# Beta's logarithm in the exponent of the decays, one tile of three decay matrices per head, and two 256-column products per chunk in place of four

## The chip, the cores and the metric

The kernel runs on one core of one Trainium2 chip. The core has a tensor engine (PE, with its weight loads PEld), a vector engine (DVE), a scalar engine (ACT), GpSimd (POOL) and a sync engine whose queue issues the DMAs (SP). They share SBUF, and PE writes to PSUM. Each engine runs its own instructions in order. The metric is the device time of one execution in microseconds; lower is better. All data is float32.

## The reference

Two layers of a diffusion backbone over 512 latent and 256 context tokens of width 1024. A layer norms and modulates the tokens, projects them, runs three mixers side by side (windowed attention, a gated DeltaNet in both directions, a Fourier mixing), merges them by gates, and ends with a squared-ReLU MLP. The change is in the DeltaNet, which has 4 heads of 128 channels. Cut to what it touches:

```python
g = jnp.cumsum(g, axis=-1)                       # log-decay within a chunk
decay = where(lower, exp(g[..., :, None] - g[..., None, :]), 0)
kb = k * beta[..., None]
a_mat = where(strict, einsum('cd,sd->cs', kb, k) * decay, 0) + eye
u, w = solve(a_mat, [v * beta, kb * exp(g)])     # unit lower triangular
qk = einsum('cd,sd->cs', qs, k) * decay          # qs = q / sqrt(128)
# scan over chunks, S the state:
v_new = u - w @ S
o = (qs * exp(g)) @ S + qk @ v_new
S = S * exp(g_last) + (k * exp(g_last - g)).T @ v_new
```

beta is a sigmoid. The backward direction is the same on flipped tokens. The kernel works with chunks of 128 tokens: 4 latent and 2 context chunks, so 6 per head.

## The kernel before, in words

A layer has three stages: a first one with the decay gates, the Fourier mixing and the first head's inputs; the mixing stage; and a main stage with gates, output projection and MLP. The mixing stage is where the changed code runs. Four Python generators are interleaved there by a nominal clock (`by_clock`): `stream_dn` runs the scan steps of a head, `stream_prep` the preparation of one head after another (`dn_prep`), `stream_na` the attention, and `stream_in` the input projections of later heads, of the attention and of 16 gate tiles. What they issue is then ordered by a planner that knows dependences, priorities and its own estimates of durations; the order on each engine, SP's queue included, is fixed before the run. Every instruction waits there for what it needs and holds what stands behind it on its engine.

Projections (`proj`, line 255) split their weights in two parts: ACT casts a weight tile to `whi` (line 243), and in the mixing stage POOL makes the remainder `wlo` (line 246), both after SP has loaded `wr` (line 240).

`gates` (from line 415) computes per token and direction the log-decay, its cumulative sum `gc` and its negative `ngc`, `beta` and products of them, as small tiles of 128 x 6 x 8; `gc` goes to DRAM (`gdr`) so that a head's row can be broadcast to all partitions.

`dn_prep` for one head, in order:
1. It takes three tiles `Df`, `Db`, `Dl` (128 x 768) from a pool `pr` with three slots, and SP loads `Df` and `Db` from `gdr` (lines 542 and 543).
2. POOL adds or subtracts the masks: `Dl` from `Df`, then `Db`, then `Df` in place (lines 549 to 551).
3. ACT takes 18 exponentials of 128x128, three per chunk, with `gc` or `ngc` as bias (lines 556 to 558).
4. For each chunk PE computes k k^T and, where there are queries, k q^T into one PSUM tile (lines 564 and 566; this PSUM tag has one buffer, shared with the later steps), and DVE multiplies them by the decays and by beta into `N` and `PT` (lines 567 to 573). In layer 1 the two context chunks have no query.
5. The diagonal 32x32 blocks of `N` go through DRAM to `Nb`, an identity is loaded to `Wb` (both in slots of `pr` again), and 31 pairs of DVE instructions invert them (lines 591 and 593). The result goes back through DRAM into `N` and `Tst`.
6. PE and ACT merge the inverses from 32 to 64 and from 64 to 128 (lines 612 to 649) with a work tile `R`, the sixth tile from `pr`; lines 643 and 645 read `R` last. ACT and DVE then copy the result to `L` (lines 652 and 653), from which the scan steps work. `N` and `L` have one buffer.

A slot of `pr` is taken again as soon as the tile in it has no reader left: the next head's `Df` comes to the slot of `Nb`, its `Db` to that of `Wb`, its `Dl` to that of `R`.

The queries `qT` and keys `kT` of a head come from `dn_in` and `l2_rope`, where POOL multiplies a rotated copy (line 505) and DVE adds (line 507). `dn_step` (from line 657) uses `PT[:, d, j]` at line 704.

Of the kernel before, what the change touches and what calls it, by code (L numbers as in the profile page):

```python
# [11 lines left out]
AF = mybir.ActivationFunctionType  # L12
# [5 lines left out]
P = 128  # L18
# [7 lines left out]
NU = 12  # L26
# [20 lines left out]
def kernel(ctx: ExitStack, tc: tile.TileContext, A: dict, out: bass.AP):  # L47
# [18 lines left out]
    def U(name, dt=F32, tag="u", w=TT):  # L66
        b, n = cur[tag]
        return b.tile([P, w], dt, tag=tag, bufs=n, name=name)
# [4 lines left out]
    @contextmanager  # L73
    def scope(name, **bufs):
        with tc.tile_pool(name=name, bufs=1, reuse_waits="tile") as b:
            for t, n in bufs.items():
                cur[t] = (b, n)
            yield b
# [42 lines left out]
    pool.memset(Tst, 0.0)  # L121
    def sigmoid_into(dst, src):

        act.activation(out=dst, in_=src, func=AF.Abs)
        act.activation(out=dst, in_=dst, func=AF.Exp, scale=-1.0)
        act.activation(out=dst, in_=dst, func=AF.Ln, bias=1.0)
        dve.scalar_tensor_tensor(dst, in0=src, scalar=0.0, in1=dst, op0=ALU.min, op1=ALU.subtract)
        act.activation(out=dst, in_=dst, func=AF.Exp)

# [245 lines left out]
    def layer(l):  # L375
# [39 lines left out]
        def gates():  # L415
# [8 lines left out]
            abv = pab[:, 0:96].rearrange("p (j c) -> p j c", c=16)  # L424
            for nm in ("z", "g", "beta", "gc", "tot", "egc", "tail", "etot", "t0", "nbe", "btail", "ngc"):
                G[nm] = sm.tile([P, 6, 8], F32, tag="g_" + nm, name="g_" + nm)
# [11 lines left out]
                                     op0=ALU.mult, op1=ALU.mult)  # L438
            sigmoid_into(G["beta"], abv[:, :, 8:16])
            pg = ps_aux("ps_g")  # L440
# [6 lines left out]
            act.copy(G["tot"], pgv[:, 2])  # L447
            dve.tensor_scalar(G["ngc"], G["gc"], -1.0, None, op0=ALU.mult)
            act.activation(out=G["egc"], in_=G["gc"], func=AF.Exp)
            act.activation(out=G["etot"], in_=G["tot"], func=AF.Exp)  # L450
# [84 lines left out]
        def dn_prep(h, st):  # L535
            kT, qT = st["kT"], st["qT"]
            v3 = lambda t: t.rearrange("p (j c) -> p j c", c=P)
            src = gdr.rearrange("(j d h) c -> h d j c", d=2, h=4)[h]
            Df = v3(U("Df", tag="pr", w=768))
            Db = v3(U("Db", tag="pr", w=768))  # L540
            Dl = v3(U("Dl", tag="pr", w=768))
            sp.dma_start(out=Df, in_=src[0].unsqueeze(0).to_broadcast([P, 6, P]))
# [9 lines left out]
            for j in range(6):  # L552
                gf = G["gc"][:, j, h:h + 1]
                ngf = G["ngc"][:, j, h:h + 1]
                ngb = G["ngc"][:, j, 4 + h:5 + h]
                act.activation(out=Dl[:, j], in_=Dl[:, j], func=AF.Exp, bias=gf, scale=-1.0)
                act.activation(out=Df[:, j], in_=Df[:, j], func=AF.Exp, bias=ngf)
                act.activation(out=Db[:, j], in_=Db[:, j], func=AF.Exp, bias=ngb)
            yield 6
            for j in range(6):  # L560
                q = full or j < 4
                tk = kT[:, j * P:(j + 1) * P]
                ps = ps_aux("ps_kk", "pp")
                pe.matmul(ps[:, 0:P], lhsT=tk, rhs=tk, start=True, stop=True)
                if q:
                    pe.matmul(ps[:, P:2 * P], lhsT=tk, rhs=qT[:, j * P:(j + 1) * P], start=True, stop=True)
                dve.scalar_tensor_tensor(N[:, 0, j], in0=ps[:, 0:P], scalar=G["beta"][:, j, h:h + 1], in1=Dl[:, j],
                                         op0=ALU.mult, op1=ALU.mult)
                dve.scalar_tensor_tensor(N[:, 1, j], in0=ps[:, 0:P], scalar=G["beta"][:, j, 4 + h:5 + h], in1=Db[:, j],
                                         op0=ALU.mult, op1=ALU.mult)  # L570
                if q:
                    dve.tensor_tensor(PT[:, 0, j], ps[:, P:2 * P], Df[:, j], op=ALU.mult)
                    dve.scalar_tensor_tensor(PT[:, 1, j], in0=ps[:, P:2 * P], scalar=G["beta"][:, j, 4 + h:5 + h],
                                             in1=Db[:, j], op0=ALU.mult, op1=ALU.mult)
                yield 1.2
# [3 lines left out]
            for b in range(4):  # L579
                s = slice(32 * b, 32 * b + 32)  # L580
                sp.dma_start(out=nd[b].rearrange("u i j -> i u j"), in_=Nu[s, :, s])
            Nb = U("Nb", tag="pr", w=1024)[0:48].rearrange("p (i j) -> p i j", j=32)
            sp.dma_start(out=Nb, in_=nd.rearrange("b u i j -> (b u) i j"))
            Wb = U("Wb", tag="pr", w=1024)[0:48].rearrange("p (i j) -> p i j", j=32)
            sp.dma_start(out=Wb, in_=A["eye32"])
# [19 lines left out]

            R = U("R", tag="pr", w=NU * 64).rearrange("p (u c) -> p u c", c=64)

# [49 lines left out]
        def dn_step(h, st, d, step):  # L657
# [36 lines left out]
            if has_q:  # L694
# [3 lines left out]
                if S is not None:  # L698
# [4 lines left out]
                    first = False  # L703
                pe.matmul(ps[:, 0:P], lhsT=st["PT"][:, d, j], rhs=Uc, start=True, stop=True)  # L704
                if first:
# [348 lines left out]
        cur["dve_lo"] = 0  # L1054
        mix_b = scope("mixb", n=8, N=1, PT=2, L=1, pr=3, sp=7, S=3, s6=6, vb=1, Pm=2, bias=2, stmp=1)
        mix_b.__enter__()
# [310 lines left out]
```

## Time and profile before

| | us |
|---|---|
| median of 3 runs | 2640.64 (2636.08 to 2641.43) |
| profiled execution | 2641.14, of which the span in the trace is 2639.4 |
| busy: PE, DVE, ACT, POOL | 2460.9, 1516.9, 1194.3, 652.1 |
| mean granted clock of PE | 0.974 |

The span runs from the first to the last instruction. The mixing stage of layer 0 lies between about 140 and 740 us, that of layer 1 between about 1600 and 2110 us. Durations of one instruction are in ns in the groups by line and in us elsewhere. A bracket behind an instruction is the idle time of its engine just before it, and what ended that.

### The profile page before, as it was taken

What the parts mean: (1) busy time and instruction counts of PE and PEld (TensorE: products, weight loads), DVE (VectorE), ACT (ScalarE), POOL (GpSimd) and SP (SyncE); (2) the same over time, 40 slices, a digit from 0 to 9 for tenths busy, and PEclk for the clock granted to TensorE, in tenths of its full rate; (3) what the DMA queues carried; (4) which work ended last, traced back from release to release, by engine and by line L of the source; (5) the groups of instructions that cost most, each with busy time, mean ns of one, the idle gap of its engine ahead of it and who ended that gap; (6) DMA issues with size and microseconds to landing.
All of it is one profiled execution on the core that took longest, in us unless ns stands there. A gap on an engine that the chain in (4) does not pass through costs nothing.

```text
span 2639.4 us, 39034 instructions
## 1 busy us (share of the span) xinstructions
PE 2460.9 (93%) x14608; PEld 2043.2 (77%) x14608; DVE 1516.9 (57%) x2867; ACT 1194.3 (45%) x2445; POOL 652.1 (25%) x552
## 2 busy tenths in 40 slices
PE   6988989989998999999999988898889999999998
PEld 3776877777887878888888867776767777788886
DVE  5628575757457976564444473858668357433334
ACT  4545656565654233131313255555565653423333
POOL 3223222231122122111111133222242232222222
PEclk9999999999998999999999999999999999999999
DMA  7223232323155733333343313232232345233332
GB/s 223 71 80 87 69 83 61 90 79 82 63 186 166 222 121 120 118 119 120 120 128 119 117 56 97 78 86 69 82 89 74 111 134 190 78 96 96 96 96 88
DMA packets 190853, 280.89 MB, mean 106 GB/s; under 512 B 57876, under 2 KB 82200, under 8 KB 190536
## 3 DMA queue, kind: packets, MB, share of 16 engines
q1 hardware_dynamic: 190664, 278.40, 34.8%
q8 instruction: 114, 1.87, 0.3%
q14 instruction: 75, 0.61, 0.1%
HBM read 242.86 MB, written 26.03 MB: 102 GB/s over the span
## 4 chain that ended last, share of the span: by engine, by line
PE 69%; DVE 15%; ACT 5%; issue 4%; DMA 3%; POOL 2%; SPq 1%; DVEq 0%; POOLq 0%; ACTq 0%
PE ps_m L255 33%; PE ps_in L255 13%; PE ps_wo L255 4%; PE ps_inc L255 4%; PE ps_br L255 3%; DVE stmp L591 2%; DVE Wb L593 2%; DVE cy L479 2%; PE ps_s L827 1%; DVE Pm L809 1%; PE ps_ch L686 1%; PE ps_ch L682 1%; DVE xn L313 1%; PE ps_ch L704 1%; PE ps_s L821 1%
## 5 line engine op out<-in xcount | busy, mean ns | idle before, releaser
L246 POOL TENSOR_TENSOR wlo<-wr,whi 128x512 fp32r<-128x512 f32 x352 | 487.0, 1385 | 1679.8 <-ACT whi L243 1555.0
L243 ACT CAST whi<-wr 128x512 fp32r<-128x512 f32 x544 | 336.0, 619 | 778.0 <-PE ps_m L255 492.2
L255 PE MATMUL ps_in<-hh,whi 128*128 128x512 f32 x960 | 381.6, 408 | 27.1 <-ACT whi L243 21.6
L255 PE MATMUL ps_in<-hh,wlo 128*128 128x512 f32 x960 | 376.0, 402 | 2.8 <-POOL wlo L246 2.6
L255 PE MATMUL ps_in<-hl,whi 128*128 128x512 f32 x960 | 376.3, 403 | 0.0
L255 PE MATMUL ps_m<-ml,whi 128*128 128x512 f32 (+1 forms) x768 | 233.5, 358 | 4.5 <-POOL ml L323 3.9
L255 PE MATMUL ps_m<-mh,whi 128*128 128x512 f32 (+1 forms) x768 | 232.9, 358 | 4.4 <-ACT mh L319 4.4
L255 PE MATMUL ps_m<-ah,whi 128*128 128x512 f32 (+1 forms) x776 | 233.6, 354 | 0.0
L255 PE MATMUL ps_m<-ah,wlo 128*128 128x512 f32 (+1 forms) x776 | 233.2, 354 | 0.0
L255 PE MATMUL ps_m<-al,whi 128*128 128x512 f32 (+1 forms) x776 | 233.0, 354 | 0.0
L255 PE MATMUL ps_m<-mh,wlo 128*128 128x512 f32 (+1 forms) x768 | 232.1, 356 | 0.0
L255 PEld LDWEIGHTS ps_in<-hh,whi 128*128 128x128 f32 x960 | 182.2, 194 | 59.2 <-ACT whi L243 23.2
L246 DVE TENSOR_TENSOR wlo<-wr,whi 128x512 fp32r<-128x512 f32 x192 | 134.8, 702 | 139.9 <-ACT whi L243 139.9
L255 PEld LDWEIGHTS ps_in<-hh,wlo 128*128 128x128 f32 x960 | 180.4, 193 | 38.6 <-POOL wlo L246 5.4
L255 PEld LDWEIGHTS ps_in<-hl,whi 128*128 128x128 f32 x960 | 181.2, 193 | 29.9 <-issue 2.2
L1197 DVE SCALAR_TENSOR_TENSOR x<-ps_m,mod,x 128x512 f32<-128x512 f32 (+1 forms) x97 | 60.8, 654 | 215.4 <-PE ps_m L255 215.4
L202 DVE SCALAR_TENSOR_TENSOR jada<-wada,csb 128x1024 f32<-128x1024 f32 x128 | 179.6, 1403 | 0.9 <-DMA wada<-in_wat_dram 0.4
L255 PEld LDWEIGHTS ps_m<-ml,whi 128*128 128x128 f32 x768 | 127.8, 189 | 29.7 <-POOL ml L323 6.8
L255 PEld LDWEIGHTS ps_m<-mh,whi 128*128 128x128 f32 x768 | 127.7, 190 | 27.3 <-ACT mh L319 6.2
L255 PE MATMUL ps_inc<-hh,whi 128*128 128x256 f32 x512 | 148.8, 291 | 0.0
L255 PE MATMUL ps_inc<-hl,whi 128*128 128x256 f32 x512 | 148.8, 291 | 0.0
L255 PE MATMUL ps_inc<-hh,wlo 128*128 128x256 f32 x512 | 148.7, 290 | 0.0
(337 smaller groups left out, 4918.3 us busy)
## 6 DMA issues: line engine op xcount, KB each, us to landing
wr<-in_w_dram SPq DMA_DIRECT2D x256, 256.0 KB, 2.6
wr<-in_wi_dram SPq DMA_DIRECT2D x224, 256.0 KB, 2.8
wada<-in_wat_dram SPq DMA_DIRECT2D x80, 512.0 KB, 4.0
wr<-in_wb_dram SPq DMA_DIRECT2D x48, 256.0 KB, 3.0
wada<-in_wa_dram SPq DMA_DIRECT2D x32, 256.0 KB, 5.4
wr<-in_wo_dram SPq DMA_DIRECT2D x32, 256.0 KB, 2.9
gpre<-sgp SPq DMA_DIRECT2D x16, 384.0 KB, 2.3
sgg<-gpre SPq DMA_DIRECT2D x16, 384.0 KB, 4.0
```

What stands on the lines that cost most here:

```text
L202: pin(dve.scalar_tensor_tensor(junk, in0=ws[n], scalar=1.0, in1=cur["csb"][:, v * D:v * D + D], op0=ALU.mult, op1=ALU.mult, accum_out=MOD[ ...
L243: act.copy(hi, raw)
L246: eng.tensor_tensor(lo, raw, hi.bitcast(F32), op=ALU.subtract)
L255: pe.matmul(ps[:, s0 - off:s1 - off], lhsT=a, rhs=b[k][:, s0:s1], start=(k == 0 and i == 0), stop=(k == kn - 1 and i == 2))
L313: dve.scalar_tensor_tensor(t[:, s0:s1], in0=xs[k][:, s0:s1], scalar=sc, in1=rs[:, s0:s1], op0=ALU.mult, op1=ALU.mult)
L479: dve.scalar_tensor_tensor(y[:, :n], in0=cin[:, j:j + n], scalar=vec[:, cw + j:cw + j + 1], in1=y[:, :n], op0=ALU.mult, op1=ALU.add)
L591: dve.tensor_tensor(tv, Nb[:, j + 1:32, j:j + 1].to_broadcast([48, n, m]), Wb[:, j:j + 1, 0:m].to_broadcast([48, n, m]), op=ALU.mult)
L593: dve.tensor_tensor(Wb[:, j + 1:32, 0:m], Wb[:, j + 1:32, 0:m], tv, op=ALU.subtract)
L682: pe.matmul(ps[:, P:2 * P], lhsT=lhs, rhs=v_t, start=True, stop=True)
L686: pe.matmul(ps[:, 2 * P:3 * P], lhsT=kt, rhs=Uc, start=True, stop=True)
L704: pe.matmul(ps[:, 0:P], lhsT=st["PT"][:, d, j], rhs=Uc, start=True, stop=True)
L1197: dve.scalar_tensor_tensor(x2[k][:, s0:s1], in0=ps[:, s0:s1], scalar=mod(l, 5, k, v), in1=x2[k][:, s0:s1], op0=ALU.mult, op1=ALU.add)
```

## The change

The logarithm of beta is kept when the sigmoid is computed (`lb`) and added to the biases of the exponentials, in a new small tile `gbl`: for the forward direction `lb + gc`, for the backward one `lb - gc`. So the decay matrices `Dl` and `Db` come out multiplied by beta, and the products need no scalar. The three matrices are laid side by side in one tile of 3072 columns, in the order `Dl`, `Db`, `Df`, so that one instruction multiplies k k^T, read twice, by `Dl` and `Db`, and one multiplies k q^T by `Db` and `Df`. For that `PT` holds its two directions the other way round, and line 704 reads `1 - d`. `Nb`, `Wb` and `R` become parts of the same tile, and the pool `pr` has one slot of 3072 columns in place of three of 1024.

```diff
--- before.py
+++ after.py
@@ -119,13 +119,14 @@
     dve.memset(ones, 1.0)
     Tst = const.tile([P, NU, P], F32, name="Tst")
     pool.memset(Tst, 0.0)
-    def sigmoid_into(dst, src):
+    def sigmoid_into(dst, src, lg=None):
 
         act.activation(out=dst, in_=src, func=AF.Abs)
         act.activation(out=dst, in_=dst, func=AF.Exp, scale=-1.0)
         act.activation(out=dst, in_=dst, func=AF.Ln, bias=1.0)
-        dve.scalar_tensor_tensor(dst, in0=src, scalar=0.0, in1=dst, op0=ALU.min, op1=ALU.subtract)
-        act.activation(out=dst, in_=dst, func=AF.Exp)
+        lg = dst if lg is None else lg
+        dve.scalar_tensor_tensor(lg, in0=src, scalar=0.0, in1=dst, op0=ALU.min, op1=ALU.subtract)
+        act.activation(out=dst, in_=lg, func=AF.Exp)
 
 
     cs = const.tile([P, KD, 32], F32, name="cs")
@@ -422,7 +423,7 @@
             for j in range(6):
                 pe.matmul(pab[:, 16 * j:16 * j + 16], lhsT=ab_f[0:32, j * P:(j + 1) * P], rhs=selab, start=True, stop=True)
             abv = pab[:, 0:96].rearrange("p (j c) -> p j c", c=16)
-            for nm in ("z", "g", "beta", "gc", "tot", "egc", "tail", "etot", "t0", "nbe", "btail", "ngc"):
+            for nm in ("z", "g", "beta", "gc", "tot", "egc", "tail", "etot", "t0", "nbe", "btail", "ngc", "gbl", "lb"):
                 G[nm] = sm.tile([P, 6, 8], F32, tag="g_" + nm, name="g_" + nm)
             alog = rows[l][:, 0:1, :].to_broadcast([P, 6, 8])
             dtb = rows[l][:, 1:2, :].to_broadcast([P, 6, 8])
@@ -436,7 +437,7 @@
             dve.scalar_tensor_tensor(G["t0"], in0=G["z"], scalar=0.0, in1=G["t0"], op0=ALU.max, op1=ALU.add)
             dve.scalar_tensor_tensor(G["g"], in0=G["t0"], scalar=-1.0, in1=ea.unsqueeze(1).to_broadcast([P, 6, 8]),
                                      op0=ALU.mult, op1=ALU.mult)
-            sigmoid_into(G["beta"], abv[:, :, 8:16])
+            sigmoid_into(G["beta"], abv[:, :, 8:16], G["lb"])
             pg = ps_aux("ps_g")
             gflat = G["g"].rearrange("p j c -> p (j c)")
             for i, m in enumerate((m_ui, m_li, ones)):
@@ -446,6 +447,9 @@
             act.copy(G["gc"][:, :, 4:8], pgv[:, 1, :, 4:8])
             act.copy(G["tot"], pgv[:, 2])
             dve.tensor_scalar(G["ngc"], G["gc"], -1.0, None, op0=ALU.mult)
+
+            dve.tensor_tensor(G["gbl"][:, :, 0:4], G["lb"][:, :, 0:4], G["gc"][:, :, 0:4], op=ALU.add)
+            dve.tensor_tensor(G["gbl"][:, :, 4:8], G["lb"][:, :, 4:8], G["gc"][:, :, 4:8], op=ALU.subtract)
             act.activation(out=G["egc"], in_=G["gc"], func=AF.Exp)
             act.activation(out=G["etot"], in_=G["tot"], func=AF.Exp)
             dve.tensor_tensor(G["t0"], G["tot"], G["gc"], op=ALU.subtract)
@@ -536,9 +540,10 @@
             kT, qT = st["kT"], st["qT"]
             v3 = lambda t: t.rearrange("p (j c) -> p j c", c=P)
             src = gdr.rearrange("(j d h) c -> h d j c", d=2, h=4)[h]
-            Df = v3(U("Df", tag="pr", w=768))
-            Db = v3(U("Db", tag="pr", w=768))
-            Dl = v3(U("Dl", tag="pr", w=768))
+
+            pr = U("pr", tag="pr", w=3072)
+            D3 = pr[:, 0:2304].rearrange("p (x j c) -> p x j c", x=3, c=P)
+            Dl, Db, Df = (D3[:, x] for x in range(3))
             sp.dma_start(out=Df, in_=src[0].unsqueeze(0).to_broadcast([P, 6, P]))
             sp.dma_start(out=Db, in_=src[1].unsqueeze(0).to_broadcast([P, 6, P]))
             N = U("N", tag="N", w=12 * P).rearrange("p (d j c) -> p d j c", d=2, c=P)
@@ -550,9 +555,9 @@
             pool.tensor_tensor(Db, Db, li, op=ALU.add)
             pool.tensor_tensor(Df, Df, ui, op=ALU.add)
             for j in range(6):
-                gf = G["gc"][:, j, h:h + 1]
+                gf = G["gbl"][:, j, h:h + 1]
                 ngf = G["ngc"][:, j, h:h + 1]
-                ngb = G["ngc"][:, j, 4 + h:5 + h]
+                ngb = G["gbl"][:, j, 4 + h:5 + h]
                 act.activation(out=Dl[:, j], in_=Dl[:, j], func=AF.Exp, bias=gf, scale=-1.0)
                 act.activation(out=Df[:, j], in_=Df[:, j], func=AF.Exp, bias=ngf)
                 act.activation(out=Db[:, j], in_=Db[:, j], func=AF.Exp, bias=ngb)
@@ -564,14 +569,10 @@
                 pe.matmul(ps[:, 0:P], lhsT=tk, rhs=tk, start=True, stop=True)
                 if q:
                     pe.matmul(ps[:, P:2 * P], lhsT=tk, rhs=qT[:, j * P:(j + 1) * P], start=True, stop=True)
-                dve.scalar_tensor_tensor(N[:, 0, j], in0=ps[:, 0:P], scalar=G["beta"][:, j, h:h + 1], in1=Dl[:, j],
-                                         op0=ALU.mult, op1=ALU.mult)
-                dve.scalar_tensor_tensor(N[:, 1, j], in0=ps[:, 0:P], scalar=G["beta"][:, j, 4 + h:5 + h], in1=Db[:, j],
-                                         op0=ALU.mult, op1=ALU.mult)
+                two = lambda t: t.unsqueeze(1).to_broadcast([P, 2, P])
+                dve.tensor_tensor(N[:, :, j], two(ps[:, 0:P]), D3[:, 0:2, j], op=ALU.mult)
                 if q:
-                    dve.tensor_tensor(PT[:, 0, j], ps[:, P:2 * P], Df[:, j], op=ALU.mult)
-                    dve.scalar_tensor_tensor(PT[:, 1, j], in0=ps[:, P:2 * P], scalar=G["beta"][:, j, 4 + h:5 + h],
-                                             in1=Db[:, j], op0=ALU.mult, op1=ALU.mult)
+                    dve.tensor_tensor(PT[:, :, j], two(ps[:, P:2 * P]), D3[:, 1:3, j], op=ALU.mult)
                 yield 1.2
 
             Nu = N.rearrange("p d j c -> p (d j) c")
@@ -579,9 +580,9 @@
             for b in range(4):
                 s = slice(32 * b, 32 * b + 32)
                 sp.dma_start(out=nd[b].rearrange("u i j -> i u j"), in_=Nu[s, :, s])
-            Nb = U("Nb", tag="pr", w=1024)[0:48].rearrange("p (i j) -> p i j", j=32)
+            Nb = pr[0:48, 0:1024].rearrange("p (i j) -> p i j", j=32)
             sp.dma_start(out=Nb, in_=nd.rearrange("b u i j -> (b u) i j"))
-            Wb = U("Wb", tag="pr", w=1024)[0:48].rearrange("p (i j) -> p i j", j=32)
+            Wb = pr[0:48, 1024:2048].rearrange("p (i j) -> p i j", j=32)
             sp.dma_start(out=Wb, in_=A["eye32"])
             tmp = U("stmp", tag="stmp", w=256)[0:48]
             yield 5
@@ -603,7 +604,7 @@
                 sp.dma_start(out=Tst[s, :, s], in_=wd[1, b].rearrange("u i j -> i u j"))
             yield 6
 
-            R = U("R", tag="pr", w=NU * 64).rearrange("p (u c) -> p u c", c=64)
+            R = pr[:, 2048:2048 + NU * 64].rearrange("p (u c) -> p u c", c=64)
 
             ps = ps_aux("ps_r", "pp")
             quads = [(q, slice(64 * q, 64 * q + 32), slice(64 * q + 32, 64 * q + 64)) for q in range(2)]
@@ -701,7 +702,7 @@
                     else:
                         dve.scalar_tensor_tensor(O, in0=ps[:, 3 * P:4 * P], scalar=col("egc"), in1=O, op0=ALU.mult, op1=ALU.add)
                     first = False
-                pe.matmul(ps[:, 0:P], lhsT=st["PT"][:, d, j], rhs=Uc, start=True, stop=True)
+                pe.matmul(ps[:, 0:P], lhsT=st["PT"][:, 1 - d, j], rhs=Uc, start=True, stop=True)
                 if first:
                     dve.tensor_copy(O, ps[:, 0:P])
                 else:
@@ -1052,7 +1053,7 @@
             sts[0]["zz"] = dn_z(0)
         psf.__exit__(None, None, None)
         cur["dve_lo"] = 0
-        mix_b = scope("mixb", n=8, N=1, PT=2, L=1, pr=3, sp=7, S=3, s6=6, vb=1, Pm=2, bias=2, stmp=1)
+        mix_b = scope("mixb", n=8, N=1, PT=2, L=1, pr=1, sp=7, S=3, s6=6, vb=1, Pm=2, bias=2, stmp=1)
         mix_b.__enter__()
         mix_p = psum("psx", **PSX)
         mix_p.__enter__()
```

## Rows read from the trace of the kernel before

**Rows 1.** The page, busy time by engine, and the chain that ended last by engine.
```profile
PE 2460.9 (93%) x14608; PEld 2043.2 (77%) x14608; DVE 1516.9 (57%) x2867; ACT 1194.3 (45%) x2445; POOL 652.1 (25%) x552
...
PE 69%; DVE 15%; ACT 5%; issue 4%; DMA 3%; POOL 2%; SPq 1%; DVEq 0%; POOLq 0%; ACTq 0%
```

**Rows 2.** Windows of both mixing stretches: length; busy us of PE, PEld, DVE, ACT, POOL; clock; DMA.
```profile
140.00:740.00 600.00, 548.80 (x3962) 460.05 (x3961) 365.20 (x880) 348.97 (x789) 152.62 (x133) 0.97 0.28 78
1600.00:2110.00 510.00, 457.60 (x3131) 365.81 (x3130) 325.11 (x782) 296.63 (x689) 152.66 (x137) 0.95 0.30 85
```

**Rows 3.** Groups by line and shape, VectorE: busy us, mean ns of one, idle before.
```profile
L567 DVE SCALAR_TENSOR_TENSOR N<-ps_kk,g_beta,Dl 128x128 f32<-128x128 f32 x48 | 16.8, 349 | 42.2 <-PE ps_kk L566 37.8 <-PE ps_tm L516 2.2 <-PE ps_kk L564 1.6
...
L569 DVE SCALAR_TENSOR_TENSOR N<-ps_kk,g_beta,Db 128x128 f32<-128x128 f32 x48 | 16.4, 342 | 0.0
...
L572 DVE TENSOR_TENSOR PT<-ps_kk,Df 128x128 f32<-128x128 f32 x40 | 11.2, 280 | 0.7 <-ACT Df L557 0.7
...
L573 DVE SCALAR_TENSOR_TENSOR PT<-ps_kk,g_beta,Db 128x128 f32<-128x128 f32 x40 | 13.6, 341 | 0.0
...
L1143 DVE TENSOR_TENSOR sgg<-sgg,ps_br 128x512 f32<-128x512 f32 x16 | 10.9, 683 | 3.5 <-PE ps_br L255 3.4
```

**Rows 4.** The chain that ended last, in order of time, head 2 of layer 0.
```profile
453.26 1.79 PE ps_inc L255 x15
```

**Rows 5.** Timeline of VectorE, gates of layer 1: start us, us.
```profile
1551.25 0.18 DVE L454 SCALAR_TENSOR_TENSOR g_nbe<-g_egc,g_beta 128x24 f32<-128x24 f32 x1
```

**Rows 6.** DMA issues: count, KB each, median us from issue to landing.
```profile
Df<-gdr SPq DMA_DIRECT2D x8, 384.0 KB, 6.5
Db<-gdr SPq DMA_DIRECT2D x8, 384.0 KB, 8.4
```

**Rows 7.** Line 645 in four windows, head 2 of layer 0, then layer 1.
```profile
L645 PE MATMUL ps_w<-N,R x12: 218/218/267, 412.6 to 413.3; 64*64 64x64 f32 x12
...
L645 PE MATMUL ps_w<-N,R x12: 311/311/362, 1739.0 to 1740.2; 64*64 64x64 f32 x12
...
L645 PE MATMUL ps_w<-N,R x12: 218/218/267, 1852.9 to 1853.6; 64*64 64x64 f32 x12
...
L645 PE MATMUL ps_w<-N,R x12: 218/218/267, 1967.4 to 1968.1; 64*64 64x64 f32 x12
```

**Rows 8.** Line 567 in the four windows that follow those.
```profile
L567 DVE SCALAR_TENSOR_TENSOR N<-ps_kk,g_beta,Dl x6: 341/350/352, 450.4 to 461.6; 128x128 f32<-128x128 f32 x6
...
L567 DVE SCALAR_TENSOR_TENSOR N<-ps_kk,g_beta,Dl x6: 336/350/351, 1748.4 to 1759.4; 128x128 f32<-128x128 f32 x6
...
L567 DVE SCALAR_TENSOR_TENSOR N<-ps_kk,g_beta,Dl x6: 341/350/351, 1861.8 to 1875.0; 128x128 f32<-128x128 f32 x6
...
L567 DVE SCALAR_TENSOR_TENSOR N<-ps_kk,g_beta,Dl x6: 350/351/351, 1982.0 to 1993.4; 128x128 f32<-128x128 f32 x6
```

**Rows 9.** Timeline of POOL around heads 1 and 3 of layer 1.
```profile
1735.44 1.80 POOL L550 TENSOR_TENSOR Db<-Db,n_li 128x768 f32<-128x768 f32 x1 [9.58 <-DMA Db<-gdr]
...
1740.66 1.83 POOL L549 TENSOR_TENSOR Dl<-Df,n_li 128x768 f32<-128x768 f32 x1 [2.19 <-issue]
...
1744.55 1.73 POOL L505 TENSOR_TENSOR rot<-rot,sinT 128x512 f32<-128x512 f32 x1
...
1977.86 1.78 POOL L505 TENSOR_TENSOR rot<-rot,sinT 128x512 f32<-128x512 f32 x1 [5.46 <-DMA rot<-kn]
```

**Rows 10.** Timeline of ACT, head 1 of layer 1.
```profile
1737.27 1.28 ACT L558 ACTIVATE Db<-Db,g_ngc 128x128 f32<-128x128 f32 x4 [5.00 <-POOL Db L550]
```

**Rows 11.** Timeline of PE: first matmul behind a wait, at four places.
```profile
163.77 0.80 PE L255 MATMUL ps_in<-hh,whi 128*128 128x512 f32 x1 [10.54 <-ACT whi L243]
...
419.73 0.80 PE L564 MATMUL ps_kk<-kT 128*128 128x128 f32 x2 [4.55 <-ACT N L649]
...
1738.96 0.36 PE L643 MATMUL ps_w<-R,N 64*64 64x64 f32 x1 [4.55 <-ACT R L640]
...
1860.52 0.80 PE L564 MATMUL ps_kk<-kT 128*128 128x128 f32 x2 [5.32 <-ACT N L649]
```

## The prediction

> **What bounds the kernel now.** I read the page's busy times first: the tensor engine (PE) works 2460.9 of 2639.4 us and carries 69% of the chain that ended last; the vector engine (DVE) carries 15% of it [rows 1]. So the change, which edits DVE work and one buffer, can win only where PE waits. The windows of the two mixing stretches, where the changed code runs, come next: PE works 548.8 of 600 us in layer 0 and 457.6 of 510 us in layer 1, which leaves 51 and 52 us of PE idle time, and DVE is busy for 61% and 64% of them [rows 2]. These 104 us are all that the change can fill; it can add to them without such a limit.
>
> The groups by line then show the products themselves. Before the first of a chunk DVE sits idle for 37.8 us in all until the matmul that it reads [rows 3]: the products wait for PE, not PE for them. In the chain, in order of time, PE puts 15 projection matmuls between the pairs of two chunks [rows 4], and no DVE piece of lines 567 to 573 stands on it. Last I read the head changes, since there the new buffer bites: the last use of R (line 645), the first product of the next head (line 567), and what POOL and ACT do between [rows 7 to 11].
>
> **Part 1, the products.** Removed are 48 + 48 + 40 + 40 instructions: per chunk 0.349 + 0.342 + 0.280 + 0.341 = 1.312 us with a query, 0.691 us without [rows 3]. Added are 88 products of 256 columns. No row has one, so I take its price from two products of the same kind with a PSUM operand: 0.280 us at 128 and 0.683 us at 512 columns [rows 3], which is 0.00105 us a column, so 0.280 + 0.134 = 0.414 us. The saving is 40 x (1.312 - 0.828) + 8 x (0.691 - 0.414) = 19.4 + 2.2 = 21.6 us. That is the ceiling, as instructions of DVE overlap a little. The floor is what surely lies on a path: the last chunk of each head, behind which the blocks of N are written out, 4 x 0.48 + 4 x 0.28 = 3 us over 8 heads. I take 4 us, near the floor, since PE and not DVE sets the pace there. Were the wide product as dear as two narrow ones, nothing is saved (a rival below).
>
> **Part 2, the gates.** Two additions of 128x24 per layer; the nearest is 0.18 us for that shape [rows 5]. Four make 0.7 us; between nothing (PE has projections to run) and that I take 0.4. A log-sigmoid that gets its own tile, and the swapped index of PT, add no instruction.
>
> **Part 3, one tile instead of three slots.** Before, the loads of the next head's Df and Db needed only the slots of Nb and Wb, and these are free once the inverses are written out; only Dl's slot waited for R. Now all three wait until R is last read, by line 645, whose time I call W: its last start plus 0.2 us, so 413.5 us for head 2 of layer 0 and 1740.4, 1853.8 and 1968.3 us for heads 1 to 3 of layer 1 [rows 7]. Behind W now come the loads (median 6.5 us for Df, 8.4 us for Db [rows 6]), two of POOL's three operations (1.83 and 1.80 us [rows 9]) and one exponential (1.28 / 4 = 0.32 us [rows 10]): 12.35 us. The earliest first products are thus 425.9, 1752.8, 1866.2 and 1980.7 us, against 450.4, 1748.4, 1861.8 and 1982.0 us before [rows 8]. In layer 0 there is room: 24.5 us at head 2, the tightest of its three changes, since those heads wait for their queries. In layer 1 heads 1 and 2 come 4.4 us late each and head 3 does not: 8.8 us, if nothing else moves.
>
> Something else does move. Before, the early Db makes ACT stop: POOL waits 9.58 us for its landing [rows 9], the exponentials of Db wait 5.00 us for POOL [rows 10], and behind them on ACT stand the last copies of the previous head. PE waits for those: 4.55, 4.55 and 5.32 us [rows 11], 14.4 us in all. The new wait forbids this order, for the exponentials cannot start before R is done; W of head 1 then comes 4.55 us sooner, its lateness is gone, and the term falls from 8.8 to 4.4 us. I take +5. Of the 14.4 us I take back a third, 4.8 us: the same 18 exponentials will still be queued ahead of the weights' casts, and where a head starts with nothing before it this cost PE 10.54 us [rows 11]. The ends are 14.4 us won and, if each of the six head changes looked like that start, 6 x 10.54 - 14.4 = 49 us lost.
>
> In SP's queue the two loads are moved behind W; weight loads that stand behind them wait with them. DVE is not held, its products wait as before; ACT's dn_step copies are what a late exponential holds.
>
> The Trainium skill ("DMA: Bandwidth & Descriptors", section "Rules for kernel authors") says to issue a DMA early, compute, and wait for it late, and this change issues two per head late. The trace agrees with it in layer 1 (8.4 us of landing against no room) and not in layer 0 (24.5 us of room). By the rule alone the landing would be paid at all six head changes; that is the last rival.
>
> **Sum.** -4 + 0.4 + 5 - 4.8 = -3.4 us. The profiled execution took 2641.1 us (span 2639.4 and 1.7 around it), 0.5 us above the median of 2640.6. So 2637.7 on its scale, 2637.2 on the median's: no change that can be measured. A measurement tells about 0.2% here, 5.3 us, so 2635.3 to 2645.9 counts as the same.
>
> **Rivals.**
> Faster, 2627 us: the hold on ACT goes without a successor, because the planner puts casts and copies ahead of exponentials that cannot be early any more. Then -14.4 - 4 + 0.4 + 4.4 = -13.6 us. For it: the three PE waits have one cause, and the change takes it away. Against: at the first head POOL and ACT stand still for the landing with nothing before it.
>
> Slower, 2657 us: POOL stands at Dl until the later landing, and behind it on the same queue is the rotation (line 505) that the next head's queries need. It starts at 1744.55 and 1977.86 us, 3.9 and 4.1 us ahead of the first products [rows 8, 9]. With three operations before it, it starts at W + 8.4 + 3 x 1.83 = W + 13.9, and the first product at W + 17.9: 1758.3 and 1986.2 us, 9.9 and 4.2 us late. Head 2, with the 9.58 us landing, is 5.6 us late. That is 19.7 us, less 4 plus 0.4: +16. It decides if the order on POOL has Dl before the rotation, and the loads are not issued before W. For it: that order stands in the trace for head 1. Against: PE has other matmuls to run meanwhile.
>
> The wide product saves nothing, 2641 us: a broadcast PSUM operand costs two passes, 0.69 us. Only a slope between other shapes speaks against it.
>
> The whole landing shows six times: 2641 + 6 x 8.4 - 4 = 2688 us. Against it speaks the room in layer 0.
>
> **How the numbers follow.** Forecast 0.34 (its own range 2632 to 2644), faster rival 0.32, slower rival 0.28, no saving 0.04, six landings 0.02. Faster by over 0.2%: the faster rival and a fifth of the forecast, 0.39. Same: the rest of the forecast and the case without a saving, 0.31. Slower: 0.30. For 8 in 10 the range goes below the faster rival by a third of the ceiling of part 1 (7 us, 2620) and just past the slower one, 2659.
>
> **What will show it.** Right: 88 products of 128x256 near 0.41 us; the loads of Df issued behind line 645 at all six head changes; no copy of R behind an exponential of Db on ACT; first products of layer 1 within 5 us of W + 12.4; layer 0's mixing stretch within a few us of 600. Wrong: PE waits at the head changes that add up to over 25 us or vanish; a first product of layer 0 that waits for an exponential; the mixing stretch of layer 1 over 10 us from 510; or a difference in the MLP stretches, which the change does not touch.

## Result and profile after

The changed kernel takes 2659.27 us (median of 4 runs, 2658.89 to 2667.88), the kernel before 2641.03 us beside it: ratio 1.0075, 95% interval 1.0056 to 1.0094. It is slower by 18 to 20 us; the forecast was 3.4 us the other way. The profiled execution took 2659.35 us, its span is 2657.6.

The page of the changed kernel, busy time by engine and the chain that ended last by engine, as [rows 1]:

```profile
PE 2469.8 (93%) x14608; PEld 2044.0 (77%) x14608; DVE 1508.4 (57%) x2783; ACT 1196.4 (45%) x2445; POOL 645.6 (24%) x552
...
PE 61%; DVE 11%; ACT 4%; issue 3%; DMA 2%; POOL 2%; SPq 0%; DVEq 0%; ACTq 0%; POOLq 0%
```

The two windows of [rows 2], now:

```profile
140.00:740.00 600.00, 545.55 (x3909) 454.74 (x3908) 351.47 (x832) 341.60 (x781) 147.44 (x132) 0.97 0.27 76
1600.00:2110.00 510.00, 452.65 (x3106) 361.64 (x3105) 322.87 (x728) 294.64 (x680) 149.58 (x138) 0.95 0.29 83
```

PE works less in the same 600 and 510 us. Measured from the end of the Fourier matmuls to the first branch matmul, the mixing stretch goes from 603.8 to 613.6 us in layer 0 and from 506.3 to 511.3 in layer 1; the stretch between them, in which the change touches only the gates of layer 1, from 862.7 to 864.9. That last difference means nothing: over all kernels of this document it lies between 859.5 and 865.0.

The new products, by line and shape, as [rows 3]:

```profile
L573 DVE TENSOR_TENSOR N<-ps_kk,pr 128x256 f32<-128x256 f32 x48 | 20.3, 424 | 55.1 <-PE ps_kk L571 37.7 <-ACT pr L563 13.4 <-ACT whi L244 2.0
L575 DVE TENSOR_TENSOR PT<-ps_kk,pr 128x256 f32<-128x256 f32 x40 | 16.6, 415 | 0.0
```

Their busy time is 36.9 us, against 16.8 + 16.4 + 11.2 + 13.6 = 58.0 before. But DVE now also waits 13.4 us for an exponential ahead of them; the row of before names none among its releasers.

The last use of R (line 646) and the first product in head 1 of layer 1, as [rows 7] and [rows 8]:

```profile
L646 PE MATMUL ps_w<-N,pr x12: 218/218/267, 1740.4 to 1741.1; 64*64 64x64 f32 x12
...
L573 DVE TENSOR_TENSOR N<-ps_kk,pr x6: 415/425/426, 1755.9 to 1765.5; 128x256 f32<-128x256 f32 x6
```

Between the two lies the chain that ended last, in order of time (start us, us, what):

```profile
1741.72 8.21 DMA pr<-gdr
1749.93 0.07 issue
1750.00 1.83 POOL pr L554
1751.83 0.07 issue
1751.90 0.47 POOL pr L556
1752.37 1.30 issue
1753.66 1.81 POOL pr L555
1755.47 0.02 issue
1755.49 0.41 ACT pr L563
1755.90 0.02 issue
1755.92 0.43 DVE N L573
1756.35 0.34 DVE PT L575
1756.69 0.14 issue
1756.82 0.77 PE ps_kk L569 x2
```

The chain cuts POOL's second operation in two; its timeline has the three back to back:

```profile
1750.00 1.82 POOL L554 TENSOR_TENSOR pr<-pr,n_li 128x768 f32<-128x768 f32 x1 [3.15 <-DMA pr<-gdr]
1751.90 1.80 POOL L556 TENSOR_TENSOR pr<-pr,n_ui 128x768 f32<-128x768 f32 x1
1753.66 1.80 POOL L555 TENSOR_TENSOR pr<-pr,n_li 128x768 f32<-128x768 f32 x1
```

This is the new wait in one piece: R is read, the load lands 8.21 us after its issue, POOL makes three matrices, ACT takes the exponential, DVE multiplies, and only then may PE have the one PSUM buffer of these steps again. Such a landing stands on the chain that ended last at four of the six head changes (6.54, 8.21, 7.58 and 6.16 us); before, it did at one (9.58 us). SP issued the first of the two loads within 1 us of the end of line 646 at all six head changes.

PE's first matmuls behind a wait at the head changes, with the idle time and its releaser in brackets, as [rows 11]:

```profile
261.36 0.76 PE L687 MATMUL ps_ch<-Uc,ktl 128*128 128x128 f32 x2 [3.69 <-ACT Uc L685]
...
424.87 0.80 PE L687 MATMUL ps_ch<-Uc,ktl 128*128 128x128 f32 x2 [6.50 <-ACT Uc L685]
...
551.84 0.79 PE L256 MATMUL ps_in<-hh,wlo 128*128 128x512 f32 x1 [2.99 <-POOL wlo L247]
562.93 0.80 PE L256 MATMUL ps_in<-hh,whi 128*128 128x512 f32 x1 [4.00 <-ACT whi L244]
...
1756.82 0.77 PE L569 MATMUL ps_kk<-kT 128*128 128x128 f32 x2 [6.14 <-DVE PT L575]
...
1868.12 0.49 PE L571 MATMUL ps_kk<-qT,kT 128*128 128x128 f32 x2 [1.05 <-DVE qT L511]
1874.82 0.77 PE L569 MATMUL ps_kk<-kT 128*128 128x128 f32 x2 [4.89 <-DVE PT L575]
...
1993.45 0.49 PE L683 MATMUL ps_ch<-Z,L 128*128 128x128 f32 x2 [1.78 <-DVE Z L681]
1998.04 0.80 PE L687 MATMUL ps_ch<-Uc,ktl 128*128 128x128 f32 x2 [3.51 <-ACT Uc L685]
```

They add up to 34.6 us; such waits come to 21 us before. Layer 0 has its share: there the state copies (`Uc`) stand behind the first of the 18 late exponentials on ACT (five of them at head 2), and the weight remainders (`wlo`) behind a POOL that waits for the landing:

```profile
420.63 0.40 ACT L561 ACTIVATE pr<-pr,g_gbl 128x128 f32<-128x128 f32 x1 [4.26 <-POOL pr L554]
...
424.58 0.24 ACT L685 COPY Uc<-ps_ch 128x128 f32<-128x128 f32 x1
...
548.77 1.80 POOL L554 TENSOR_TENSOR pr<-pr,n_li 128x768 f32<-128x768 f32 x1 [5.00 <-DMA pr<-gdr]
550.52 1.26 POOL L247 TENSOR_TENSOR wlo<-wr,whi 128x512 fp32r<-128x512 f32 x1
```

### The profile page after: what moved, and what is told of

Same layout as the page of the kernel before. It is cut to its first block, busy times and chain, and to the rows that moved or that the text cites. A ratio compares the mean times of both kernels' runs of the same rounds, so it can differ in the third digit from the quotient of the medians.

```text
span 2657.6 us, 38993 instructions
## 1 busy us (share of the span) xinstructions
PE 2469.8 (93%) x14608; PEld 2044.0 (77%) x14608; DVE 1508.4 (57%) x2783; ACT 1196.4 (45%) x2445; POOL 645.6 (24%) x552
## 4 chain that ended last, share of the span: by engine, by line
PE 61%; DVE 11%; ACT 4%; issue 3%; DMA 2%; POOL 2%; SPq 0%; DVEq 0%; ACTq 0%; POOLq 0%
PE ps_m L256 33%; PE ps_in L256 10%; PE ps_wo L256 4%; PE ps_br L256 3%; PE ps_inc L256 2%; DVE stmp L592 2%; DVE cy L483 2%; DVE pr L594 1%; DMA pr<-gdr 1%; DVE xn L314 1%; PE ps_br L1101 1%; DVE Pm L810 1%; PE ps_s L828 1%; PE ps_ch L687 1%; DVE jada L203 1%
```

## Experiments

Seventeen further kernels were measured. "Mix" is the change of the mixing stretch in the profiled run against before, layer 0 and layer 1, in us; the median of before lay between 2640.5 and 2643.6 us. The profiled runs of a_rown_narrow, a_p3 and a_pre_p2 lay 8 to 13 us below the medians of these kernels, so their stretches are on the short side.

| kernel | median us | ratio to before, 95% | mix |
|---|---|---|---|
| b_one | 2666.35 | 1.0092 (1.0077 to 1.0106) | +20.3, +6.9 |
| a_rown | 2658.68 | 1.0059 (1.0047 to 1.0071) | +0.5, +12.4 |
| a_narrow | 2652.87 | 1.0039 (1.0026 to 1.0052) | +7.2, +1.2 |
| a_later | 2667.80 | 1.0099 (1.0084 to 1.0113) | +12.7, +9.2 |
| b_log | 2667.41 | 1.0104 (1.0085 to 1.0122) | +21.6, +2.6 |
| a_once | 2654.39 | 1.0050 (1.0035 to 1.0066) | -2.1, +9.4 |
| a_rown_narrow | 2658.92 | 1.0062 (1.0039 to 1.0085) | +1.8, +6.0 |
| b_logstt | 2647.53 | 1.0018 (1.0006 to 1.0030) | +5.8, -0.8 |
| a_noload2 | 2637.85 | 0.9978 (0.9965 to 0.9991) | -6.1, -0.6 |
| b_p2 | 2649.80 | 1.0025 (1.0011 to 1.0039) | +10.2, -1.2 |
| a_p2 | 2658.69 | 1.0057 (1.0037 to 1.0077) | +12.4, +2.1 |
| a_pre | 2637.76 | 0.9979 (0.9967 to 0.9992) | -4.1, -1.7 |
| a_pre_n | 2649.13 | 1.0024 (1.0012 to 1.0036) | +5.6, +2.2 |
| b_p3 | 2636.65 | 0.9982 (0.9971 to 0.9993) | +2.6, -6.0 |
| a_p3 | 2652.65 | 1.0041 (1.0024 to 1.0057) | +1.9, 0.0 |
| a_pre_p2 | 2646.97 | 1.0014 (1.0000 to 1.0028) | -7.7, -2.2 |
| a_pre_p3 | 2640.34 | 0.9995 (0.9985 to 1.0006) | -1.1, -3.9 |

**The buffer alone, in before's code (b_one).**

```diff
+            pr = U("pr", tag="pr", w=3072)
+            Dl, Db, Df = (v3(pr[:, 768 * x:768 * x + 768]) for x in range(3))
...
-  mix_b = scope(..., pr=3, ...)
+  mix_b = scope(..., pr=1, ...)
```

> The kernel before with its four scalar products and its gates as they were; only the three slots of 1024 columns become one tile of 3072, laid out as in the changed kernel. Theory A (the single tile makes the next head's loads wait for R, and PE then stands still at the head changes): as slow as the changed kernel, 2655 to 2665 us, and PE's waits at the six head changes add up to 30 us or more against 21 us before. Rival B (the cost is in the products, the log of beta or the new order of the work they bring): 2641 us, within 5 us.

23 us longer: the layout loses without any new product or gate. Its longest PE wait at a head change of layer 0, 7.41 us before a projection at 564.16, ended on POOL's `wlo`; the longest of layer 1, 8.12 us at 2004.89, on a state copy of ACT.

**R in a buffer of its own (a_rown), and with narrow products (a_rown_narrow).**

```diff
-            pr = U("pr", tag="pr", w=3072)
+            pr = U("pr", tag="pr", w=2304)
-            R = pr[:, 2048:2048 + NU * 64]...
+            R = U("R", tag="rr", w=NU * 64)...
```

> The changed kernel with R in a tile of its own (768 columns) and the shared tile cut to 2304: same bytes, but the loads of Df and Db wait only until the inverses of the 32x32 blocks are written out. Theory A: the loads go out some 15 us ahead of line 646 again and the time falls back to 2641 us or below it, 2628 to 2643. Rival B: 2655 to 2662 us, since products and gates are those of the changed kernel.

The time is B's, but b_one, where nothing but the buffer and the order differs, speaks against B, and the place is new: layer 0 is back at its length of before, and layer 1 loses 12.4 us. The loads now come early. PE waits 4.23 and 4.50 us for copies of R (before 1727.74 and 1848.67), and these stand on ACT behind the sigmoid of an input projection (lines 124 to 126), which waits for a convolution on DVE:

```profile
1724.90 0.63 ACT L124 ACTIVATE cin<-cy 128x512 f32<-128x512 f32 x1 [5.96 <-DVE cy L483]
...
1726.76 0.93 ACT L616 COPY R<-ps_r 32x384 f32<-32x384 f32 x2
```

The decay's own exponentials come behind these copies. So these two waits have nothing to do with the landing; they come with the order. What else makes up the 12.4 us is open.

> R in a buffer of its own, the three decays in another, and four plain 128-column products. If wide products cost by themselves (B): about 6 us less than with R apart and wide products, so 2650 to 2655. If the width is nothing and only the order that the planner finds differs (A): 2656 to 2661, with layer 1's mixing stretch still about 12 us longer than before.

No difference that can be told: its runs spread from 2647.96 to 2664.44.

**Narrow products (a_narrow).**

```diff
-   dve.tensor_tensor(N[:, :, j], two(ps[:, 0:P]), D3[:, 0:2, j], op=ALU.mult)
+   for x in range(2):
+       dve.tensor_tensor(N[:, x, j], ps[:, 0:P], D3[:, x, j], op=ALU.mult)
```

> The changed kernel with four products of 128 columns per chunk in place of two of 256. Theory A: the products lie beside PE's work, 2659 us within 5 us. Rival B (wide products are the cost): 2641 to 2650 us. Had the products been worth what their durations say (40 x 0.29 + 8 x 0.14 us, from 0.280 us narrow and 0.414 wide), it would be 13 us slower, 2672 us.

10 us above before, between the theories, and 9 to 10 below the changed kernel by the ratios. I took that for a cost of the wide products; the later pairs don't bear it out (below).

**A pause behind the two loads (a_later).**

```diff
             sp.dma_start(out=Db, in_=src[1]...)
+            yield 6
```

> The changed kernel with six units of the nominal clock between the two loads and what POOL and ACT do with them, so that scan steps, casts and copies that are due in between are put ahead of the exponentials. If the loss is what stands behind the exponentials on ACT and POOL (A, hold): 2645 to 2652 us, with PE's waits at the head changes under 20 us. If it is that the next head's products come later (A, lateness): 2659 us or above, up to 2675. Rival B: no change, 2659 us.

Later work loses more (26 us). That speaks for lateness, and against a cost only of what stands queued behind the early POOL operations; but the pause makes a new order too, and one run does not tell the two apart.

**Before's three slots with the logarithm (b_log), and before's places in one tile with wide products (a_once).**

```diff
-  pr = U("pr", tag="pr", w=3072)            # b_log: three U(..., tag="pr", w=768) again
+  if h == 0: cur_pr[0] = U("pr", tag="pr", w=3072)   # a_once: Dl|R, Db|Wb, Df|Nb
```

> Three slots as before, beta's logarithm in the exponent, four plain 128-column products per chunk. Theory A (all of the loss comes from the one buffer, which holds the loads of the decays until R is read): 2634 to 2644, L0's mixing stretch ends as before, and the four products get cheaper by 1.312 - 4 x 0.28 = 0.19 us a chunk, of which next to nothing shows. Rival B (the new biases, or what the planner makes of the changed products, cost by themselves): 2648 or more.

> The wide products and the logarithm as in the changed kernel, but one buffer for the whole stage, whose parts are taken again one by one: Df in the columns of Nb, Db in those of Wb, Dl in those of R, as the three slots were. Theory A (the late loads are the loss, the wide products cost nothing): 2632 to 2644, loads issued before line 645 and the first products back at the times of before. Rival B (the wide products cost PE about 6 us by themselves, as the run with narrow ones was 6 us shorter): 2645 to 2652.

b_log was the surprise: no buffer shared with R, and 27 us lost. The planner sees other durations for the products and finds another order, from the first head of layer 0 on. Its timeline of ACT in that order, where the next head's exponentials stand ahead of the second copy of R (start us, us, wait in brackets):

```profile
544.81 0.47 ACT L643 COPY R<-ps_r 64x384 f32<-64x384 f32 x1 [0.60 <-PE ps_r L641]
551.29 1.28 ACT L563 ACTIVATE Db<-Db,g_gbl 128x128 f32<-128x128 f32 x4 [5.63 <-POOL Db L555]
552.48 0.45 ACT L643 COPY R<-ps_r 64x384 f32<-64x384 f32 x1
```

and PE behind it:

```profile
552.99 0.37 PE L646 MATMUL ps_w<-R,N 64*64 64x64 f32 x1 [5.00 <-ACT R L643]
```

This wait is the landing again (POOL stands idle for 11.63 us before `Db`, until its load is there), met at another place; but the kernel before has waits of this kind and size [rows 11], so it does not explain the 21.6 us of layer 0. a_once has the loads of before and the wide products and still loses 13 us, in layer 1. So order is a term of its own, and a layout can't be judged by one order.

**The logarithm in before's order (b_logstt).**

```diff
-   scalar=G["beta"][:, j, h:h + 1]
+   scalar=ones[:, 0:1]                       # biases from gbl
```

> Beta's logarithm in the exponent with before's three slots, and the products left as scalar_tensor_tensor with a scalar of one, so that the planner sees the durations of before; PE, ACT, POOL and SP issue in the order of before. Theory O (the order that the planner finds is what costs: the run with three slots and plain products, 27 us longer, had another order from PE's 571st row on): 2637 to 2645. Theory L (the logarithm itself costs, by larger biases or a later gate): 2655 to 2668.

4 us (0.06% to 0.30%) longer, 23 less than b_log: the logarithm costs next to nothing, the order of b_log about 20 us. The time lies just above theory O's range and well below L's. PE, ACT and POOL do issue in before's order, instruction by instruction. In the profiled run PE's idle time in layer 0's stretch is 49.1 us against 51.2 before, its busy time 560.5 against 552.6, at a mean granted clock of 0.955 against 0.975: what is left there is slower matmuls.

**The landing left out (a_noload2).**

```diff
+            if h == 0: cur_dx[0] = ...; sp.dma_start(out=cur_dx[0], in_=src[0]...)
-            pool.tensor_tensor(Dl, Df, li, op=ALU.subtract)
+            pool.tensor_tensor(Dl, Dx, li, op=ALU.subtract)      # Db, Df likewise
```

> The changed kernel without the six later pairs of loads of the decays: heads 1 to 3 of a layer take head 0's row and biases, and the backward matrix is made as the forward one, so the decays of those heads are left out. POOL and ACT still wait for R. Theory H (the landing behind R is the loss): POOL's Dl starts within 1 us of R's last use, the time is 2632 to 2646. Theory O (the order is the loss, the landing a small part): 2648 to 2665.

The time is that of theory H: 2637.85, 21 us below the changed kernel by the medians, 25 by the ratios. Waiting for R costs nothing here by itself. But without the loads the planner finds another order: 988 of PE's 14608 matmuls, from the 1389th on, stand at another place than in the changed kernel. This run alone does not tell the landing from the order.

**The rows loaded ahead (a_pre), and with narrow products (a_pre_n).** Nothing is left out here.

```diff
-  pr = U("pr", tag="pr", w=3072)
+  pr = U("pr", tag="pr", w=2304)             # R in the columns of Nb
+  Dx = U("Dx", tag="dx", w=1536)...
-  sp.dma_start(out=Df, in_=src[0]...)        # Db likewise
+  sp.dma_start(out=Dx[:, 0], in_=src[0]...)
-  pool.tensor_tensor(Dl, Df, li, op=ALU.subtract)
+  pool.tensor_tensor(Dl, Dx[:, 0], li, op=ALU.subtract)
```

> The changed kernel, but the two rows of a head are loaded ahead into a tile of their own (1536 columns), from which POOL makes the three matrices once R is read; R lies in the columns of Nb, so the one buffer shrinks to 2304 columns and room is found. Theory H (the landing behind R is what the change loses): all loads of heads 1 to 3 are issued long before line 645, POOL's Dl starts within 1 us of R's last use, 2633 to 2645, near the run without the loads (2638). Theory O (the order decides): 2648 to 2665, as with the two nearest layouts (2654, 2659).

> The same with four plain 128-column products in place of the two wide ones. If the landing is the loss and the width is nothing (H): within 5 us of the wide one. If narrow products are better by themselves, as in the one pair so far (6 us): 2627 to 2637. If only the order differs (O): anywhere from 2640 to 2665.

a_pre takes 2637.76 us and beats both kernels in this order: 0.2% below before (interval 0.08% to 0.33%). On PE, ACT, POOL and DVE it issues in the very order of a_noload2, and takes the same time: the loads themselves cost nothing once they are early. It is thus no second witness against the order. Line 647 is its last use of R, at head 2 of layer 0:

```profile
L647 PE MATMUL ps_w<-N,pr x12: 218/218/267, 409.8 to 410.5; 64*64 64x64 f32 x12
```

and POOL makes Dl 0.4 us after the last of these starts. In the changed kernel the last starts at 411.2 and POOL at 418.80, 7.6 us later. POOL in a_pre:

```profile
410.90 1.85 POOL L555 TENSOR_TENSOR pr<-Dx,n_li 128x768 f32<-128x768 f32 x1 [8.43 <-PE ps_w L647]
```

and SP, which already loads the rows of the head after, 117 us before POOL reads them at 533.4:

```profile
416.65 0.37 SPq L548 DMA_DIRECT2D Dx<-gdr  x1
```

What tells the landing from the order is PE's busy time in the 40 us behind the last use of R, at the six head changes of each kernel (240 us in all; columns as in [rows 2]). The changed kernel:

```profile
sum 240.00, PE 203.19 PEld 169.96 DVE 120.28 ACT 142.00 POOL 82.21; mean PE 33.87 PEld 28.33 DVE 20.05 ACT 23.67 POOL 13.70
```

and a_pre:

```profile
sum 240.00, PE 216.12 PEld 178.99 DVE 143.68 ACT 150.66 POOL 97.54; mean PE 36.02 PEld 29.83 DVE 23.95 ACT 25.11 POOL 16.26
```

and before:

```profile
sum 240.00, PE 216.05 PEld 180.63 DVE 144.57 ACT 143.83 POOL 82.86; mean PE 36.01 PEld 30.10 DVE 24.10 ACT 23.97 POOL 13.81
```

So the change makes PE idle for 12.9 us more there. Six kernels issue these loads behind the last use of R (the changed one, b_one, a_narrow, a_later, and a_p2 and a_p3 below), each in an order of its own: PE works 198.7 to 204.9 us in them. In the thirteen others, whose loads come earlier or are left out, it works 213.5 to 226.0 us. None of these orders closes the gap. The whole time is not parted so cleanly: the six lie 10 to 26 us above before, the others between 6 us below and 27 us above it (the two kernels with R apart, a_once and b_log lose elsewhere).

a_pre_n is 12 us above a_pre. Over four pairs narrow less wide is -10 (a_narrow), +1 (a_rown_narrow), +14 (b_log less a_once, not quite the same tiles) and +12 us (a_pre_n): no sign that outlives the order.

**Two other orders.** One nominal time of the planner's clock is changed, in before (b_), in the changed kernel (a_) and in a_pre; nothing else is.

```diff
-IN_T, LAT_STEP, HEAD, PRI, GR, G0 = (12, 7), (2, 3), (5, 0), ...
+... (2.2, 3.2), (5, 0)    # p2
+... (2, 3), (6, 1)        # p3
```

> The kernel before with one nominal time of the planner's clock changed by a tenth (LAT_STEP 2, 3 to 2.2, 3.2): no instruction is added or removed, only the order differs. Theory O: any other order costs, 2648 to 2668. Theory H: the order is nearly nothing, 2636 to 2647.

> The changed kernel with the same nominal time changed by a tenth. Theory O: it lands anywhere between 2640 and 2675, and its distance to the kernel before with the same nominal time is not 18 us. Theory H: 2655 to 2664, 15 to 22 us above the kernel before with the same nominal time.

> The kernel before with another nominal time of the planner's clock changed (HEAD 5, 0 to 6, 1): order alone. Theory O as it stands after the first such run (6 us longer): 2643 to 2660. If the first was chance: 2637 to 2645.

> The changed kernel with the same nominal time changed. If the landing costs by itself, in any order (H): 10 to 22 us above the kernel before with the same nominal time. If order is nearly all (O): the distance may have either sign.

> The changed kernel with its rows loaded ahead, and the nominal time of the second order (LAT_STEP 2.2, 3.2). Theory H (the landing costs 15 to 21 us in any order): 13 us or more below the changed kernel in the same order (2659), so 2637 to 2646, and below the kernel before in it (2650). Theory O (its gain in the first order was that order's luck): 2648 to 2662.

> The same with the nominal time of the third order (HEAD 6, 1). Theory H: 2631 to 2640, 13 us or more below the changed kernel in that order (2653) and not above the kernel before in it (2637). Theory O: 2643 to 2658.

In us by the ratios, against the kernel before in its own order:

| | order of the text | p2 | p3 |
|---|---|---|---|
| before | 0 | +7 | -5 |
| changed | +20 | +15 | +11 |
| changed, rows loaded ahead | -6 | +4 | -1 |
| changed less before | +20 | +8 | +16 |
| landing: changed less loaded ahead | +25 | +11 | +12 |
| rest: loaded ahead less before | -6 | -3 | +3 |

A line of the upper part has an interval of 3 to 5 us to either side, a difference one of 3 to 7. In each setting the three kernels also differ in what the planner made of it, so the row of the landing holds its order as well. It is positive in all three, with zero outside the interval; what is left of the change without it is nothing that outlives the order. H holds in sign, in a smaller size than the first order showed: its 15 us or more between a_p2 and b_p2 came out as 8, and its 13 us or more between the changed kernel and the one loaded ahead as 11 and 12; a_pre_p3 is not below b_p3 but 3 us above. b_p3 at 2636.65 is faster than either theory had it. Of O this much holds, that an order is worth 5 to 7 us here and about 20 in b_log. Which of b_log's many moves cost these 20 us was not tried.

## Why the prediction was wrong

**What bounds the kernel: right.** PE sets the pace, and the change could win or lose only where PE waits.

**Products and gates: right.** A wide product takes 0.424 and 0.415 us, forecast 0.414; 58.0 - 36.9 = 21.1 us of DVE time are saved, forecast 21.6, and as foreseen almost none of it shows: the change without its landing is at -6 to +3 us, orders included, forecast -3.6. The additions to the biases took 0.18 us each.

**The late landing: half right.** From the end of line 646 to the first product I had 12.35 us. It is 14.6 and 14.5 us at heads 1 and 2 of layer 1 (1741.3 to 1755.9, 1859.4 to 1873.9): three POOL operations stand there in place of two, and the load goes out 0.4 and 0.9 us after the end. At head 3, which I had as not late, it is 22.4 us (1980.36 to 2002.75) against 13.7 before: there the query itself is late. Its normalisation (`r_l`) stands on ACT behind exponentials that wait for the landing, and POOL's rotation (line 509) follows:

```profile
1988.90 0.99 ACT L561 ACTIVATE pr<-pr,g_gbl 128x128 f32<-128x128 f32 x3 [4.24 <-POOL pr L554]
1989.80 0.57 ACT L498 ACTIVATE r_l<-ps_l 128x512 f32<-128x512 f32 x1
...
1997.13 1.27 POOL L509 TENSOR_TENSOR rot<-rot,sinT 128x512 f32<-128x512 f32 x1 [4.54 <-DMA rot<-kn]
```

**"In layer 0 there is room" failed.** I measured the room at the first product (24.5 us at head 2), which waits for its query anyway. The landing does not only hold the products. It holds POOL, with `wlo` behind it, and ACT, with `Uc` and weight casts behind the late exponentials; these belong to the previous head's scan and to the projections, and they had no room. The waits of 3.69, 6.50, 2.99 and 4.00 us in layer 0 are theirs.

**The step that failed most is the 4.8 us taken back.** Before's three waits (14.4 us, [rows 11]) did go: no copy of the previous head (R at line 640, N at line 649) stands behind an exponential of Db any more. But I let a third of them be won, where the same late exponentials made new waits at all six head changes, 34.6 us against 21 before. The end that I worked out for this, 49 us lost, was the right direction. In the sum, +5 - 4.8 let PE idle for 0.2 us more at the head changes; it idles 12.9 us more in the 40 us behind the last uses of R, and the time of the landing, late products and order included, is 25 us in this order and 11 to 12 in two others. As a sign of being wrong I had waits that add up to over 25 us; they did, but the 21 us of before show that the mark said little.

**The rivals.** The slower one had the size (+16) by luck, on a wrong way: it put the rotation behind Dl, but at heads 1 and 2 of layer 1 the rotation of the changed kernel ran at 1745.11 and 1863.53, ahead of Dl at 1750.00 and 1867.98. At head 3 it did run behind all three POOL operations, but what it waited for was its own load, made late by ACT. Its 9.58 us for head 2 is POOL's idle time at head 1 [rows 9]. And it put all of the loss in layer 1, where 5 of the 15 us of both stretches are. The six whole landings (50 us) were too many: 25, 11 and 12 us were measured. The Trainium skill ("DMA: Bandwidth & Descriptors", section "Rules for kernel authors") asks for a DMA to be issued early and waited for late. The runs agree with it: loading the rows ahead does just that and gets the 11 to 25 us back, order included; the size doesn't follow from the rule.

**Not in the forecast at all:** that a change of a duration or a dependence can make the planner find a new order. By itself that moved the kernel before by +7 and -5 us, more than the -3.4 us that I was working out.

## What to carry to other kernels

When buffers are merged, list for each part the load that was free to start and now waits for the last reader of another part; then ask not who needs the data, but what stands behind the operation that waits for it on its in-order engine. Give such a load a landing place of its own, even if the matrices made from it stay in the shared buffer: 6 KB per partition did it here. And where an order is planned, compare a change in several orders before you believe a difference of 10 us.

## What the hardware showed

A long wait of PE can be paid twice. Behind the 6.50 us wait the granted clock of the changed kernel was 0.63 for 5 us and 1.00 after that, as it had been until the wait (windows; the clock is the number behind POOL's):

```profile
410.00:418.00 8.00, 7.91 (x75) 6.97 (x74) 1.85 (x5) 5.52 (x14) 0.00 (x0) 1.00 0.38 127
425.00:430.00 5.00, 5.00 (x26) 4.87 (x27) 2.69 (x9) 3.59 (x13) 0.46 (x1) 0.63 0.18 52
430.00:435.00 5.00, 5.00 (x33) 4.37 (x32) 4.79 (x9) 2.91 (x10) 1.27 (x1) 1.00 0.01 3
```

0.63 is a mix of the two levels, 1.2 and 2.4 GHz, for part of the stretch each. Layer 0's mixing stretch grew by 9.8 us, of which 6.1 are PE's busy time (552.6 to 558.7 us; the kernels have 14608 matmuls each) and 3.7 its idle time (51.2 to 54.9). Its mean granted clock fell from 0.975 to 0.967, which is worth some 5 us (an estimate: the share that was not granted, times the length of the stretch, before and after). In layer 1 the 5.0 us are idle time alone (53.2 to 58.5; busy 453.1 and 452.8, clock 0.949 and 0.947). So a forecast that counts idle time alone can be too small.
